# Attention weights times V as three float32r products of split operands, in place of one float32 product

## The chip, the core and the metric

The kernel runs on one core of one Trainium2 chip. The metric is the device time of one execution in microseconds (us). Engines are named as in the profile: PE (TensorE matmul), PEld (its weight load), DVE (VectorE), ACT (ScalarE), POOL (GpSimd), SP (SyncE, which issues the DMAs).

## The reference

Two layers of a decoder trunk on 256 tokens of width 1024, all in float32. Each layer projects the normed input into three branches (a gated depthwise convolution of 31 taps, a sparse attention, a short gated convolution), merges them with gates, and ends with a feed-forward block. The part that matters here is the attention, for each block of 128 queries:

```python
logits = jnp.einsum('btgrd,btkgd->btgrk', qg, kg).astype(jnp.float32) * scale
logits = jnp.where(valid[:, :, None, None, :], logits, -jnp.inf)
p = jax.nn.softmax(logits, axis=-1).astype(v.dtype)
o = jnp.einsum('btgrk,btkgd->btgrd', p, vg)
```

There are 8 query heads in 2 groups, each group with one key and one value head of 128 columns.

## The kernel before

**Streams.** The weights arrive as chunks of 2048 columns by 128 rows. Each chunk is cut into two halves of 1024 columns. ACT rounds a half to float32r (`cast`, L429, tile `wh`), DVE subtracts that from the original (`low`, through `vtt`, L386, tile `wl`). There are six buffers of `wh` and six of `wl`. The activations are split in the same way, and each product with a weight tile is three float32r matmuls: high by high, low by high, high by low. A half of 1024 columns holds 8 tiles and so feeds 24 matmuls of 256 columns. Each layer takes 180 halves; 90 of them come before the stage `T` of the layer.

**Stages of a layer**, in the order of the weights: `A` (convolution branch in), `IQ`, `KX`, `V`, `Q` (attention in), `C`, `CB`, `S` (short branch), `G` (gates), `T` (attention out), `F` (convolution branch out), `O`, `U`, `N` (feed-forward). Beside them run the convolution (`acc`, 31 taps on DVE with a third of the taps prepared by ACT as `ct`) and the attention itself, both fed into the other stages' gaps.

**Order.** No order is left to the hardware: `Plan.schedule` gives every instruction a cost and a due time, and on each engine takes next, among the instructions that are ready at that moment, the one with the smallest due time. It puts out one fixed order for each engine. The due time of a matmul group is the running sum `clk["t"]` of PE costs; that of a weight half's `cast` and `low` is `clk["t"] - LEAD` (9 us before its use); that of all convolution taps is one constant, the layer's start plus `CONVDUE` (150 us); attention steps get a due time of their own, advanced by `spend`.

**Attention loop.** For each of 2 query blocks `b` and 2 groups `g` there are: float32 products `qk`, a masked row maximum on DVE (L968, `lgt`), the softmax on ACT, a transposition on PE of each key block (`tp`, L367; one key block for `b`=0, two for `b`=1), an ACT copy of it to SBUF (`pT`), and the product with V:

```python
po = G.buf([P, 4, P], "pa", f"po{l}_{b}_{g}")
pe([mm(po, vt[:, kb, g * P:(g + 1) * P], pT[kb], kb == 0, kb == b, 512, True)
    for kb in range(b + 1)])
act(ah[:, hs, bq], po, AF.Copy)
low(al[:, hs, bq], po, ah[:, hs, bq])
```

Each product has 128 rows and 512 columns. Over both layers there are 12: per layer one for each of the two groups of `b`=0, two for each group of `b`=1. The result `ah`, `al` is read by stage `T`. `vt` is an ACT copy of the V projection. Line numbers of helpers: L369 is every matmul, L386 `vtt`, L393 `vstt` (convolution taps and others), L424 `act`, L429 `cast`.

Of the kernel before, what the change touches and what calls it, by code (L numbers as in the profile page):

```python
# [10 lines left out]
F32R = mybir.dt.float32r  # L11
I32 = mybir.dt.int32
AF = mybir.ActivationFunctionType
# [3 lines left out]
P = 128  # L17
D = 1024
S = 256
# [40 lines left out]
for _n, _w in (("ident", 128), ("caus0", 128), ("caus1", 256), ("cosq", 32), ("sinq", 32),  # L60
# [4 lines left out]

SLOTS = {"raw": 3, "wh": 6, "wl": 6, "big": 8, "att": 2, "pm": 4, "pq": 2, "pa": 2,
         "m1": 5, "m2": 3, "rr": 3, "b1": 2, "b2": 2, "lgt": 1, "rel": 2, "rope": 4, "junk": 1,
         "m8": 2, "tv": 3, "ty": 3, "tt": 3, "r2": 2, "two": 7, "one": 9, "mx": 2, "sm": 2, "ri": 2}
SHARED = {"m1": ("one", 5), "rr": ("one", 3), "b1": ("one", 2), "m2": ("two", 3), "rel": ("two", 2), "b2": ("two", 2), "ct": ("two", 2)}
BANKS = ("pm", "pq", "pa")  # L70
LAYOUT = (["gap40"] + [f"big_{i}" for i in range(8)] + [f"att_{i}" for i in range(2)] + ["kT_0", "vt_0"],
# [68 lines left out]
def ap_of(x):  # L140
    return x.ap() if isinstance(x, View) else x
# [198 lines left out]
def trunk(ctx: ExitStack, tc: tile.TileContext, xt: bass.AP, wst: bass.AP, prm: bass.AP,  # L340
# [7 lines left out]
    G = Plan()  # L348
    clk = {"t": 0.0}

    def width(v):
        if isinstance(v, View) and not v.whole:
            return v.n
        raise ValueError

    def pe(mms, due=None):
        outs, ins, cost = {}, {}, 0.0
        for o, l, r, st, sp, n, full, kw in mms:
            outs[id(o)] = o
            ins[id(l)] = l  # L360
            ins[id(r)] = r
            cost += max(4 * (n / 2.4 + 1.2), 218) if full else max(n, 256) / 2.4 + 2.4

        def fn():
            for o, l, r, st, sp, n, full, kw in mms:
                if kw == "t":
                    nc.tensor.transpose(ap_of(o), ap_of(l), ap_of(r))  # L367
                else:
                    nc.tensor.matmul(ap_of(o), ap_of(l), ap_of(r), start=st, stop=sp, skip_group_check=bool(kw))  # L369

        G.add("pe", fn, list(outs.values()), list(ins.values()), cost, due=due)
        return cost

    def mm(o, l, r, st, sp, n, full=False, kw=None):
        return (o, l, r, st, sp, n, full, kw)

    def tr(o, i):
        return (o, i, ident, True, True, P, False, "t")

    def psum(v):  # L380
        return isinstance(v, View) and v.buf.tag in BANKS

    def vtt(o, a, b, op, n=None):
        n = n or width(o)
        c = 62 if psum(a) or psum(b) or psum(o) else 66
        G.add("dve", lambda: nc.vector.tensor_tensor(ap_of(o), ap_of(a), ap_of(b), op=op), [o], [a, b], (c + n) / 0.96)  # L386
# [20 lines left out]
    def act(o, i, f, scale=None, bias=None, accum=None, n=None):  # L407
        n = n or width(o)
        cost = n / 1.2 + (51 if psum(i) else 94)
        kw = {}  # L410
        ins = [i]
        outs = [o]
        for k, v in (("scale", scale), ("bias", bias)):
            if v is not None:
                kw[k] = v
                ins.append(v)
                cost += 93
        if accum is not None:
            kw["accum_out"] = accum
            outs.append(accum)  # L420
            cost += 93

        def fn():
            nc.scalar.activation(ap_of(o), ap_of(i), f, **{k: ap_of(v) for k, v in kw.items()})  # L424

        G.add("act", fn, outs, ins, cost, func=f)
# [8 lines left out]
    def low(o, full, hi):  # L435
        vtt(o, full, hi.bitcast(F32), ALU.subtract)
# [16 lines left out]
    def big(name, dt=F32, tag="big"):  # L453
        return G.buf([P, 8, S], tag, name, dt)
# [91 lines left out]
    for k in range(KD):  # L546
        r, src = (r0, src0) if k < 4 else (r1, src1)
        dma(r[:, 512 * (k % 4):512 * (k % 4 + 1)], src[:, 512 * (k % 4):512 * (k % 4 + 1)], 256, -9e5)
        if k in (0, 1, 2, 4, 6):
            w = 1 if k < 2 else 2  # L550
# [90 lines left out]
    def tok(name, xh, xl, n, chunks):  # L641
        one = n * 2 <= 512
        if one:
            t = G.buf([P, 2, n], "pm", name)
            ps = [t[:, b, :] for b in range(2)]
        else:
            t = [G.buf([P, n], "pm", f"{name}_{b}") for b in range(2)]
            ps = t
        per = KD // (2 * chunks)
        for c in range(chunks):  # L650
            base = 2 * W.c
            for k0 in range(2 * c * per, 2 * (c + 1) * per, per):
                h, l = W.get(base + k0 // per - 2 * c)
                g = []
                for k in range(k0, k0 + per):
                    o = k % per * n
                    for b in range(2):
                        sl = slice(b * P, (b + 1) * P)
                        st = k == 0 and (b == 0 or not one)
                        g.append(mm(ps[b], xh[k][:, sl], h[:, o:o + n], st, False, n, kw="s"))  # L660
                        g.append(mm(ps[b], xh[k][:, sl], l[:, o:o + n], False, False, n, kw="s"))
                        g.append(mm(ps[b], xl[k][:, sl], h[:, o:o + n], False, k == KD - 1, n, kw="s"))
                clk["t"] += pe(g, due=clk["t"])
            W.skip()
        G.due = clk["t"]
        return t
# [96 lines left out]
    for l in range(DEPTH):  # L763
# [38 lines left out]
        ikT = G.buf([P, S], "ikT", f"ikT{l}")  # L802
        iws = G.buf([P, 2, IH], "iws", f"iws{l}")
        kx = G.buf([P, 2, KX], "kx", f"kx{l}")
        vt = G.buf([P, 2, S], "vt", f"vt{l}")
        iqb = big(f"iq{l}")
        ssq = G.buf([P, 2, HEADS], "ssq", f"ssq{l}")
        rs = G.buf([P, 2, HEADS], "rs", f"rs{l}")
# [17 lines left out]
        for t in range(0, 4, 2):  # L826
            pt = G.buf([P, 2, S], "pq", f"tiq{l}_{t}")
# [4 lines left out]
        pt = G.buf([P, S], "pq", f"tik{l}")  # L832
# [16 lines left out]
        pt = G.buf([P, 2, S], "pa", f"tk{l}")  # L849
# [1 line left out]
        act(kT, pt, AF.Copy, scale=par("kgm"))  # L851

        psv = tok(f"V{l}", xh, xl, 256, 1)
        act(vt, psv, AF.Copy)

        qt = big(f"qt{l}")
        qr = qt.rearrange("p (b h) (u d) -> p b (h u) d", b=2, u=2)
# [2 lines left out]
        for g in range(2):  # L860
# [12 lines left out]
            for i in range(2):  # L873
                pt = G.buf([P, 2, S], "pa", f"tq{l}_{n + i}")
# [8 lines left out]
        def spend(ns):  # L883
            paced["t"] += ns * PACE
            G.due = paced["t"]

        for b in range(2):
            nk = (b + 1) * P
            one = (66 + nk) / 0.96
# [5 lines left out]
            g = []  # L895
# [8 lines left out]
            for c in range(4 // per):  # L904
                for i in range(2):
                    rl = G.buf([P, per, nk], "rel", f"rel{l}_{b}_{c}_{i}")
                    act(rl, pss[c][i], AF.Relu)
                    for u in range(per):
                        h = 2 * (per * c + u) + i
# [3 lines left out]
            for r in range(TOPK // 8):  # L913
                m8 = G.buf([P, 8], "m8", f"m8{l}_{b}_{r}")
# [34 lines left out]
        for b in range(2):  # L949
            nk = (b + 1) * P  # L950
            one = (66 + nk) / 0.96
            bq = slice(b * P, (b + 1) * P)
            for g in range(2):
                G.due = paced["t"]
                mx = G.buf([P, 4], "mx", f"mx{l}_{b}_{g}")
                sm = G.buf([P, 4], "sm", f"sm{l}_{b}_{g}")
                ri = G.buf([P, 4], "ri", f"ri{l}_{b}_{g}")
                lgt = G.buf([P, 4, nk], "lgt", f"lgt{l}_{b}_{g}")
                hs = slice(4 * g, 4 * g + 4)
                pss = []  # L960
                for hp in range(2):
                    ps = G.buf([P, 2, nk], "pq", f"qk{l}_{b}_{g}_{hp}")
                    pe([mm(ps[:, i, :], qT[:, 4 * g + 2 * hp + i, bq], kT[:, g, :nk], True, True, nk, True)
                        for i in range(2)])
                    for i in range(2):
                        u = 2 * hp + i
                        G.add("dve", lambda o=lgt[:, u, :], i=ps[:, i, :], m=mx[:, u:u + 1], bb=bias[b]:
                              nc.vector.tensor_tensor_reduce(ap_of(o), ap_of(i), ap_of(bb), 1.0, GONE,  # L968
                                                             ALU.add, ALU.max, ap_of(m)),
                              [lgt[:, u, :], mx[:, u:u + 1]], [ps[:, i, :], bias[b]], one)  # L970
                spend(4 * one)
                vstt(mx, mx, -1.0, rs[:, b, hs], ALU.mult, ALU.mult)
                for u in range(4):
                    act(lgt[:, u, :], lgt[:, u, :], AF.Exp, scale=rs[:, b, 4 * g + u:4 * g + u + 1],
                        bias=mx[:, u:u + 1], accum=sm[:, u:u + 1])
                G.add("dve", lambda ri=ri, sm=sm: nc.vector.reciprocal(ap_of(ri), ap_of(sm)), [ri], [sm], 100)
                for u in range(4):
                    act(lgt[:, u, :], lgt[:, u, :], AF.Copy, scale=ri[:, u:u + 1])
                spend(500)
                pT = []  # L980
                for kb in range(b + 1):
                    pt = G.buf([P, 4, P], "pa", f"tp{l}_{b}_{g}_{kb}")
                    pe([tr(pt[:, u, :], lgt[:, u, kb * P:(kb + 1) * P]) for u in range(4)])
                    s = G.buf([P, 4, P], "b2", f"pT{l}_{b}_{g}_{kb}")
                    act(s, pt, AF.Copy)
                    pT.append(s)
                spend(500)
                po = G.buf([P, 4, P], "pa", f"po{l}_{b}_{g}")
                pe([mm(po, vt[:, kb, g * P:(g + 1) * P], pT[kb], kb == 0, kb == b, 512, True)
                    for kb in range(b + 1)])  # L990
                act(ah[:, hs, bq], po, AF.Copy)
                low(al[:, hs, bq], po, ah[:, hs, bq])
                spend(700)
# [224 lines left out]
```

## Time and profile before

| what | value |
|---|---|
| median of 3 runs | 1032.6 us (1032.03 to 1032.61) |
| the profiled execution, its own time | 1033.92 us |
| its span, first to last instruction | 1032.1 us |
| granted TensorE clock | 1.00 of full speed throughout |
| PE / PEld / DVE / ACT busy | 1025.4 / 1003.1 / 910.3 / 697.6 us |

The span is 1.8 us shorter than the execution's own time; what lies outside it is not touched. The busy time of PE is a modelled one: matmuls overlap, so a matmul that shows 276 ns may follow the one before it after 113 ns. What a matmul costs is therefore read from runs of many, as the chain gives them, by dividing time by count. The same holds for DVE, where the next instruction may begin before the one before it has ended: the distance between starts is what an instruction costs.

### The profile page before, as it was taken

The page shows a single profiled execution, that of the slowest core. Times are in us where ns is not written, and L with a number is a line of the kernel's source. Part 1 is how long each engine was busy: PE and PEld are TensorE (multiplying, and loading weights), DVE is VectorE, ACT ScalarE, POOL GpSimd, SP SyncE. Part 2 cuts the span into 40 slices and gives each one's busy share as a digit, 9 for nine tenths or more (in the row PEclk, how much of TensorE's full clock was granted, in tenths as well). Part 3 has the DMA queues.
Part 4 walks back from the last instruction along what each step waited for, and adds up shares of the span by engine and source line. Part 5 has one row for each costly group of instructions (what it writes and reads, how often), then busy time and mean ns, then how long its engine had stood idle before and what let it go on. Part 6 is the DMA issues. An engine that isn't in the chain of part 4 may idle for free.

```text
span 1032.1 us, 21274 instructions
## 1 busy us (share of the span) xinstructions
PE 1025.4 (99%) x8584; PEld 1003.1 (97%) x8584; DVE 910.3 (88%) x1805; ACT 697.6 (68%) x1228; POOL 0.2 (0%) x4
## 2 busy tenths in 40 slices
PE   8999999999999999999999999999999999999998
PEld 8998999999999999999999989999999999999998
DVE  6999999999998899885689999999998789998742
ACT  6878758896566676665476796588957466776531
POOL 0000000000000000000000000000000000000000
PEclk9999999999999999999999999999999999999999
DMA  8564445345665356555545544643564653655550
GB/s 307 204 235 185 166 160 173 123 159 169 238 207 204 124 204 227 196 206 200 182 173 195 205 161 160 210 159 124 170 238 164 211 198 128 226 220 193 186 215 21
DMA packets 29187, 191.59 MB, mean 186 GB/s; under 512 B 3232, under 2 KB 4512, under 8 KB 6816
## 3 DMA queue, kind: packets, MB, share of 16 engines
q1 hardware_dynamic: 28656, 189.70, 52.2%
q8 instruction: 67, 1.10, 0.4%
q10 hardware_dynamic: 432, 0.53, 0.2%
q14 instruction: 32, 0.26, 0.1%
HBM read 189.17 MB, written 1.05 MB: 184 GB/s over the span
## 4 chain that ended last, share of the span: by engine, by line
PE 96%; DVE 2%; DMA 1%; ACT 0%; issue 0%; ACTq 0%; SPq 0%
PE U L369 23%; PE G L369 13%; PE N L369 12%; PE C L369 9%; PE A L369 6%; PE Q L369 4%; PE T L369 4%; PE S L369 4%; PE CB L369 4%; PE O L369 4%; PE F L369 4%; PE IQ L369 2%; PE KX L369 1%; PE V L369 1%; PE qk L369 1%; PE po L369 1%
## 5 line engine op out<-in xcount | busy, mean ns | idle before, releaser
L386 DVE TENSOR_TENSOR wl<-raw,wh 128x1024 fp32r<-128x1024 f32 (+2 forms) x364 | 433.8, 1201 | 62.7 <-ACT wh L429 62.0
L429 ACT CAST wh<-raw 128x1024 fp32r<-128x1024 f32 (+2 forms) x364 | 369.5, 1030 | 139.2 <-PE N L369 37.1
L369 PE MATMUL U<-hhb,wh 128*128 128x256 f32 x576 | 134.1, 276 | 0.0
L369 PE MATMUL U<-hhb,wl 128*128 128x256 f32 x576 | 134.1, 276 | 0.0
L393 DVE SCALAR_TENSOR_TENSOR acc<-a,psb,acc 128x246 f32<-128x246 f32 (+16 forms) x320 | 132.4, 464 | 0.2
L369 PEld LDWEIGHTS U<-hhb,wh 128*128 128x128 f32 x576 | 108.1, 188 | 0.0
L369 PEld LDWEIGHTS U<-hhb,wl 128*128 128x128 f32 x576 | 108.1, 188 | 0.0
L369 PE MATMUL G<-hha,wh 128*128 128x256 f32 x384 | 90.4, 278 | 0.0
L369 PE MATMUL G<-hha,wl 128*128 128x256 f32 x384 | 89.7, 276 | 0.0
L369 PE MATMUL N<-uh,wh 128*128 128x256 f32 x352 | 80.7, 276 | 0.0
L369 PE MATMUL N<-uh,wl 128*128 128x256 f32 x352 | 80.7, 276 | 0.0
L369 PE MATMUL U<-hlb,wh 128*128 128x256 f32 x576 | 77.0, 276 | 0.0
L393 DVE SCALAR_TENSOR_TENSOR u<-U,psb,u 128x255 f32<-128x255 f32 (+1 forms) x144 | 59.7, 475 | 14.4 <-ACT u L424 14.4
L369 PEld LDWEIGHTS G<-hha,wl 128*128 128x128 f32 x384 | 72.1, 188 | 0.2 <-issue 0.2
L369 PEld LDWEIGHTS G<-hha,wh 128*128 128x128 f32 x384 | 72.1, 188 | 0.2 <-issue 0.2
L369 PEld LDWEIGHTS U<-hlb,wh 128*128 128x128 f32 x576 | 70.6, 188 | 0.0
L424 ACT ACTIVATE ct<-a,psb 128x253 f32<-128x253 f32 (+9 forms) x160 | 70.2, 488 | 0.0
L369 PEld LDWEIGHTS N<-uh,wh 128*128 128x128 f32 x352 | 66.1, 188 | 0.0
L369 PEld LDWEIGHTS N<-uh,wl 128*128 128x128 f32 x352 | 66.1, 188 | 0.0
L369 PE MATMUL C<-hha,wh 128*128 128x256 f32 x256 | 60.6, 279 | 0.0
L369 PE MATMUL C<-hha,wl 128*128 128x256 f32 x256 | 60.0, 276 | 0.0
L424 ACT ACTIVATE u<-U,psb 128x256 f32<-128x256 f32 x72 | 37.3, 560 | 27.3 <-PE U L369 27.3
(255 smaller groups left out, 2487.5 us busy)
## 6 DMA issues: line engine op xcount, KB each, us to landing
raw<-in_w SPq DMA_DIRECT2D x174, 1024.0 KB, 4.8
raw<-in_w SPq DMA_DIRECT2D x4, 656.0 KB, 3.8
raw<-in_w SPq DMA_DIRECT2D x8, 256.0 KB, 5.2
out<-xres SPq DMA_DIRECT2D x8, 128.0 KB, 2.8
psb<-in_p SPq DMA_DIRECT2D x2, 277.0 KB, 6.7
xres<-in_xt SPq DMA_DIRECT2D x2, 256.0 KB, 4.9
csb<-in_c SPq DMA_DIRECT2D x1, 304.0 KB, 8.9
xres<-in_xt ACTq DMA_DIRECT2D x1, 256.0 KB, 6.8
```

The costliest lines, as they stand in the source:

```text
L369: nc.tensor.matmul(ap_of(o), ap_of(l), ap_of(r), start=st, stop=sp, skip_group_check=bool(kw))
L386: G.add("dve", lambda: nc.vector.tensor_tensor(ap_of(o), ap_of(a), ap_of(b), op=op), [o], [a, b], (c + n) / 0.96)
L393: G.add("dve", lambda: nc.vector.scalar_tensor_tensor(ap_of(o), ap_of(a), ap_of(s), ap_of(b), op0=op0, op1=op1), [o], [a, s, b], (c + n) / ...
L424: nc.scalar.activation(ap_of(o), ap_of(i), f, **{k: ap_of(v) for k, v in kw.items()})
L429: G.add("act", lambda: nc.scalar.copy(ap_of(o), ap_of(i)), [o], [i], width(o) / 1.2 + 94)
```

## The change

V and the transposed softmax weights are each split into a float32r part and the rest, as the weights and activations already are, and the float32 product becomes three float32r products into the same PSUM tile. The V projection's copy is now the high part, and DVE makes the low part `vl` (a subtraction of 512 columns, once a layer). The ACT copy of each transposed block is now its high part, and DVE makes its low part from PSUM (512 columns, once for each key block). Two buffers `pl` and one `vl` are new in SBUF. No DMA is touched.

```diff
-         "m8": 2, "tv": 3, ...
+         "m8": 2, "pl": 2, "tv": 3, ...
...
-        vt = G.buf([P, 2, S], "vt", f"vt{l}")
+        vh = G.buf([P, 2, S], "vt", f"vh{l}", F32R)
+        vl = G.buf([P, 2, S], "vl", f"vl{l}", F32R)
...
-        act(vt, psv, AF.Copy)
+        act(vh, psv, AF.Copy)
+        low(vl, psv, vh)
...
-                    s = G.buf([P, 4, P], "b2", f"pT{l}_{b}_{g}_{kb}")
-                    act(s, pt, AF.Copy)
-                    pT.append(s)
+                    h = G.buf([P, 4, P], "b2", f"pTh{l}_{b}_{g}_{kb}", F32R)
+                    w = G.buf([P, 4, P], "pl", f"pTl{l}_{b}_{g}_{kb}", F32R)
+                    act(h, pt, AF.Copy)
+                    low(w, pt, h)
+                    pT.append((h, w))
...
-                pe([mm(po, vt[:, kb, g * P:(g + 1) * P], pT[kb], kb == 0, kb == b, 512, True)
-                    for kb in range(b + 1)])
+                gs = slice(g * P, (g + 1) * P)
+                mms = []
+                for kb in range(b + 1):
+                    h, w = pT[kb]
+                    mms.append(mm(po, vh[:, kb, gs], h, kb == 0, False, 512))
+                    mms.append(mm(po, vl[:, kb, gs], h, False, False, 512))
+                    mms.append(mm(po, vh[:, kb, gs], w, False, kb == b, 512))
+                pe(mms)
```

## Rows read from the trace of the kernel before

**Rows 1.** The page: busy time of each engine, and the chain by engine.
```profile
PE 1025.4 (99%) x8584; PEld 1003.1 (97%) x8584; DVE 910.3 (88%) x1805; ACT 697.6 (68%) x1228; POOL 0.2 (0%) x4
...
PE 96%; DVE 2%; DMA 1%; ACT 0%; issue 0%; ACTq 0%; SPq 0%
```

**Rows 2.** Waits before PE, first and last of four (us in total, times, longest).
```profile
PE A L369 <- ACT xgha L424: 1.1, 1, 1.1
...
PE A L369 <- DVE wl L386: 0.6, 2, 0.4
```

**Rows 3.** Instructions on the tile po: ns min/median/max, first and last start.
```profile
L369 PE MATMUL po<-pT,vt x24: 590/592/592, 171.3 to 742.3; 128*128 128x512 f32 x24
```

**Rows 4.** Timeline of PE around one product of layer 0: start, length, instruction.
```profile
171.26 1.02 PE L369 MATMUL po<-pT,vt 128*128 128x512 f32 x2
...
172.23 0.28 PE L369 MATMUL CB<-hha,wl 128*128 128x256 f32 x1
```

**Rows 5.** The chain in order of time, three pieces: start, length, matmul count.
```profile
72.26 2.80 PE V L369 x24
...
78.96 10.97 PE Q L369 x48
...
347.14 112.48 PE U L369 x992
```

**Rows 6.** Engines' busy us in stretches of layer 0 (PE, PEld, DVE, ACT).
```profile
80.00:90.00 10.00, 10.00 (x47) 8.21 (x46) 9.48 (x20) 7.75 (x15) 0.00 (x0) 1.00 0.51 179
...
160.00:205.00 45.00, 45.00 (x373) 43.63 (x373) 44.83 (x106) 38.83 (x87) 0.00 (x0) 1.00 0.41 141
...
231.00:262.00 31.00, 31.00 (x276) 31.00 (x275) 30.75 (x53) 19.68 (x31) 0.00 (x0) 1.00 0.50 173
```

**Rows 7.** Timeline of DVE in layer 0: start, length, instruction, [idle before].
```profile
209.69 0.69 DVE L386 TENSOR_TENSOR al<-po,ah 128x512 fp32r<-128x512 f32 x1
210.29 0.64 DVE L386 TENSOR_TENSOR acc<-acc,ct 128x470 f32<-128x470 f32 x1
...
212.76 1.23 DVE L386 TENSOR_TENSOR wl<-raw,wh 128x1024 fp32r<-128x1024 f32 x1
...
231.25 0.69 DVE L386 TENSOR_TENSOR al<-po,ah 128x512 fp32r<-128x512 f32 x1 [0.83 <-ACT ah L424]
...
243.31 1.22 DVE L386 TENSOR_TENSOR wl<-raw,wh 128x1024 fp32r<-128x1024 f32 x1
...
245.95 0.68 DVE L386 TENSOR_TENSOR mg<-g,mg 128x512 f32<-128x512 f32 x1
...
247.11 1.22 DVE L386 TENSOR_TENSOR wl<-raw,wh 128x1024 fp32r<-128x1024 f32 x1
...
259.54 1.22 DVE L386 TENSOR_TENSOR wl<-raw,wh 128x1024 fp32r<-128x1024 f32 x1
...
293.95 0.75 DVE L386 TENSOR_TENSOR cfl<-lu,cfh 128x256 fp32r<-128x256 f32 x2
```

**Rows 8.** The chain in layer 0 from the third attention step to stage T.
```profile
207.93 18.14 PE G L369 x160
...
230.58 35.36 PE G L369 x312
...
266.37 6.38 PE G L369 x56
272.75 3.63 PE T L369 x32
```

**Rows 9.** The chain in layer 1, first gate run and start of stage T.
```profile
715.76 20.86 PE G L369 x184
...
782.77 1.81 PE T L369 x16
```

**Rows 10.** Timeline of DVE in layer 1 at the same place.
```profile
716.42 0.69 DVE L386 TENSOR_TENSOR al<-po,ah 128x512 fp32r<-128x512 f32 x1 [0.72 <-ACT ah L424]
...
724.58 1.22 DVE L386 TENSOR_TENSOR wl<-raw,wh 128x1024 fp32r<-128x1024 f32 x1
```

More of the change, by code (lines that the diff above doesn't have):

```diff
@@ L67 @@
          "m1": 5, "m2": 3, "rr": 3, "b1": 2, "b2": 2, "lgt": 1, "rel": 2, "rope": 4, "junk": 1,
-         "m8": 2, "tv": 3, "ty": 3, "tt": 3, "r2": 2, "two": 7, "one": 9, "mx": 2, "sm": 2, "ri": 2}
+         "m8": 2, "pl": 2, "tv": 3, "ty": 3, "tt": 3, "r2": 2, "two": 7, "one": 9, "mx": 2, "sm": 2, "ri": 2}
 SHARED = {"m1": ("one", 5), "rr": ("one", 3), "b1": ("one", 2), "m2": ("two", 3), "rel": ("two", 2), "b2": ("two", 2), "ct": ("two", 2)}
```

## The prediction, before the change was run

> **What bounds the kernel now.** I read the page first, then who waited for whom, then the chain of waits, and last the timelines of DVE and PE side by side. The page and the chain say PE: 99% busy, 96% of the chain [rows 1]. The waits before PE are four, and both rows shown are of stage A; none lies behind the first stage [rows 2]. From there to the end PE runs without a gap, so a microsecond of matmul taken away is a microsecond of the whole, as long as PE's operands stay ahead. That condition is the question here, for DVE, which makes the low half of every weight, is full in the very stretch that the change touches: 44.83 of 45 us from 160 on and 30.75 of 31 from 231 on [rows 6].
>
> How far ahead is DVE? The trace doesn't number the halves, but they can be counted back from stage T. A half feeds 24 matmuls, 24 x 0.1134 = 2.72 us (0.1134 = 112.48 / 992, [rows 5]). 90 halves precede T, the first four of them written in two pieces each, so T's first half is the 95th `wl` write; that of 259.54 us is the 91st, four halves before T: 96 G matmuls. Of these 56 run from 266.37 us and 40 end the run before, which ends at 230.58 + 35.36 = 265.94 [rows 8]. The first reads at 265.94 - 40 x 0.1134 = 261.4 us. The DVE instruction ends at 259.54 + 1.22 = 260.76 [rows 7]. **The lead is 0.6 us.** The same count for the `wl` of 212.76 us (20 halves, 480 of the 544 G matmuls from 207.93 on, so read at 207.93 + 64 x 0.1134 = 215.2, written by 213.99): 1.2 us [rows 7, 8]. In layer 1 the smallest lead in this stretch is that of 724.58 us: 19 halves before T, 456 of the 560 G matmuls between 715.76 and 782.77, so read at 715.76 + 104 x 0.1134 = 727.55, written by 725.80: 1.7 us [rows 9, 10]. So PE is the bound with DVE directly behind it.
>
> **What the change takes from PE.** A float32 product shows as two matmul instructions [rows 3]. The pair starts at 171.26, and the second matmul behind it at 172.23, one of 0.113 after the first [rows 4]: the product holds PE for 0.86 us. Over 12 products that is 10.3 us. The three float32r products of 512 columns have no row of their own with these operands. The nearest is stage Q, also 512 columns of float32r: 10.97 / 48 = 0.2285 [rows 5]. The bounds: a quarter of the float32 product, 0.2145, and twice stage V's 256 columns, 2 x 2.80 / 24 = 0.233. With 0.2285 a product becomes 0.686, saves 0.174, and 12 save **2.1 us** (bounds 1.9 to 2.6). Stage U would say 2 x 0.1134, inside them.
>
> The Trainium skill ("FP8 and Floating Point Precision", TensorE Precision Notes) says that true float32 takes four passes through the array, and reduced precision reads the value cut to 22 bits in one. By that rule alone three passes cost three quarters, which saves 12 x 0.215 = 2.6 us. The trace agrees in kind, but stage Q's pass is slower than a float32 pass, so I take the smaller figure.
>
> **What it adds to DVE.** Per layer six lows of transposed weights and one of V, each a subtraction of 512 columns with a PSUM operand. The same shape and kind stands in the trace as `al`: 0.69 us long, 0.60 from start to start (209.69 to 210.29, [rows 7]). So 14 x 0.60 = 8.4 us. The V low comes at about 80 us, where DVE was idle for 0.52 us of ten [rows 6]; I cost it at nothing, and at 0.6 if that cover is gone. The six others fall between 168 and 231 us in layer 0, and at the corresponding place in layer 1.
>
> The Trainium skill ("VectorE: DVE Perf Modes", § TRN2 errata) gives (N+151)/0.96 ns for a float32 tensor_tensor, 0.69 us at 512 columns, and its tier table leaves float32 tensor_tensor in the slowest mode. The trace's length agrees; by the page's figure the sum would be 14 x 0.69 = 9.7 us, and the six in a layer would weigh 0.5 us more, but the distance between starts is what the queue pays.
>
> Who is behind them? Due times decide. The attention's due times are smaller than those of the weight halves used at the time, and the convolution's one due time is past, so `wl` comes last: it gets a turn only where a convolution step waits for the one before it. The row of `mg` at 245.95 between two `wl` shows another step taking such a turn [rows 7]. The lows will go ahead of `wl`, not behind.
>
> **ACT, buffers, the new wait.** ACT does the same copies in another output type: nothing. `po` now waits for a DVE low behind the ACT copy, 0.6 us plus whatever DVE has in hand (a `wl`, 1.13). Behind `po` on PE stand gate matmuls of the fixed order; the planner places `po` after the low's planned end, so I cost this at nothing, and at 8 x 1.7 = 14 us if all eight steps ran into it. `ah` is not needed before T, some 40 us later. `pl` and `vl` touch no transfer.
>
> **The sum.** Layer 0: by 259.54 six lows have gone ahead, 6 x 0.60 = 3.6 us; the lead covers 0.6, and the idle 0.83 us ahead of `al` at 231.25 [rows 7] may or may not absorb some, since the new lows wait for PE in the same way. PE is late by 2.2 to 3.0 us, I take 2.6. The 1.05 us that PE saves in this layer is gone too, because PE then waits for DVE whatever it did before. At 215.2 us four lows against 1.2 us already give 1.2 us of this. Past that point it is not lost twice: the convolution branch's last low (293.95, ends 294.70, [rows 7]) is read only in the fifth microsecond of F, and F begins later as well.
>
> Layer 1: at 724.58 four lows are ahead, 2.4 us, against a lead of 1.7 and an idle 0.72 [rows 10]: PE late by 0 to 0.7. Then the last two products give 0.35 back: -0.35 to +0.35, I take 0. Between the layers DVE recovers.
>
> Together +2.6 us (1.85 to 3.35): 1032.1 + 2.6 = 1034.7 of span, 1036.5 for the profiled execution with its 1.8 us outside the span. That execution lies 1.3 us above the median of the runs, so against the median: **1035.2 us**.
>
> **The rivals.**
>
> *The saving stays* (faster). If the planner leaves the weight halves ahead, PE keeps its 2.1 us: 1030.5 (1030.0 to 1030.7). For it: PE waits for nothing now [rows 2], and convolution steps could go later. It decides only if about 3.6 us of convolution (nine taps) moves behind the halves read at 215 and 261 us. Against it: the convolution's due time is past. Chance 0.20.
>
> *The two cancel.* The planner hides about half of the lows; PE waits 0.2 to 2.9 us in all and saves 2.1: 1030.7 to 1033.4. Chance 0.17.
>
> *The lows take turns, not only time.* Each low that takes a gap between two dependent convolution steps sends the `wl` there to the next gap; `wl` of 243.31 to the next at 247.11 shows 3.8 us where `mg` took one [rows 7], about 2.2 us each way without it. Two lows in front of the half at 215 and two in front of those after 231 then cost 4 to 7 us in layer 0 and up to 2 in layer 1: 1036.7 to 1041.5, the middle 1038.5. Against it: if PE is late, the gate steps come later too and free their turns. Chance 0.18.
>
> *The forecast*, DVE late by the plain sum of its work. Its bottom is 1.2 us of lateness at the half read at 215 alone, less 0.35 in layer 1: 1033.4. Its top is 3.35 and an uncovered V low of 0.6: 1036.6. Chance 0.45.
>
> **How the numbers follow.** 0.2% of 1032.6 is 2.1 us, about what a measurement of this kernel can tell from no change. The saving by itself sits on that edge: of its 0.20, 0.11 is faster and 0.09 the same. The cancelling case is the same (0.17). The forecast lies beyond 1034.7 in three parts of five: 0.27 slower, 0.18 the same. The last rival is slower. In all 0.11 faster, 0.44 the same, 0.45 slower. The range leaves out about a tenth at either end: 1030.3 cuts the lower half of the saving's case, 1038.5 the upper half of the last rival's. The forecast's own range is 1033.4 to 1036.6.
>
> **What would show it.** Right: waits of PE for `wl` in stages S or G of layer 0 between 190 and 262 us, 2 to 4 us in sum, none or few in layer 1; 36 `po` matmuls 0.21 to 0.235 us apart; 14 more DVE subtractions 0.60 apart. Wrong: no wait of PE behind stage A (the saving stays), or waits of 5 us and more with `wl` several turns later (the last rival), or `po` itself waiting for its low, which would make it slower at another place.

## The result and the profile after

The changed kernel takes **1040.2 us** (median of 4, 1038.54 to 1040.42); beside it the kernel before took 1032.61 (4 runs, 1032.03 to 1032.91). The ratio is 1.0067, interval 1.0055 to 1.0080: slower by 7.6 us, where 1035.2 was forecast with a range up to 1038.5. The profiled execution took 1040.42 us, its span is 1038.6.

The page of the changed kernel, busy times and chain, against [rows 1]:

```profile
PE 1027.2 (99%) x8596; PEld 1009.5 (97%) x8596; DVE 917.7 (88%) x1819; ACT 698.7 (67%) x1228; POOL 0.2 (0%) x4
...
PE 82%; DVE 14%; ACT 3%; issue 1%; DMA 0%; DVEq 0%; ACTq 0%
```

PE has the 12 new matmuls and DVE the 14 new subtractions (7.4 us more). The busy shares hardly move; the chain does: DVE goes from 2% of it to 14%. The waits before PE, against [rows 2], say where:

```profile
PE G L369 <- DVE wl L386: 6.1, 4, 2.2
PE A L369 <- ACT xgha L424: 1.2, 1, 1.2
PE pw L369 <- DVE avg L535: 1.0, 1, 1.0
```

Four waits of stage G for the low half of a weight, 6.1 us, which the kernel before did not have. The chains of both kernels give the stretch in which the time is lost: the first piece of V (before's first one is in [rows 5]) and of F in each layer, before and then after.

```profile
295.46 21.76 PE F L369 x192
...
581.99 2.81 PE V L369 x24
...
805.02 21.76 PE F L369 x192
```

```profile
70.71 2.81 PE V L369 x24
...
298.33 21.76 PE F L369 x192
...
584.86 2.80 PE V L369 x24
...
811.53 21.76 PE F L369 x192
```

From V to F the kernel before needs 295.46 - 72.26 = 223.20 us in layer 0 and 805.02 - 581.99 = 223.03 in layer 1; the changed one 227.62 and 226.67. That is **+4.42 and +3.64**. From F to the next V both need 286.53. So everything is lost between V and F, where the attention is. (The profiled execution of before began V 1.55 us later, which is why the spans differ by 6.5 and not by 8.1.)

**The mechanism, half by half.** DVE in layer 0, against [rows 7]: the stretch between two turns of `wl`.

```profile
204.43 1.21 DVE L386 TENSOR_TENSOR wl<-raw,wh 128x1024 fp32r<-128x1024 f32 x1
205.56 0.64 DVE L386 TENSOR_TENSOR acc<-acc,ct 128x482 f32<-128x482 f32 x1
206.13 0.67 DVE L386 TENSOR_TENSOR pTl<-tp,pTh 128x512 fp32r<-128x512 f32 x1
206.73 1.58 DVE L393 SCALAR_TENSOR_TENSOR acc<-a,psb,acc 128x240 f32<-128x240 f32 x4
208.24 0.67 DVE L386 TENSOR_TENSOR pTl<-tp,pTh 128x512 fp32r<-128x512 f32 x1
208.84 0.63 DVE L386 TENSOR_TENSOR acc<-acc,ct 128x476 f32<-128x476 f32 x1
209.41 0.41 DVE L970 CUSTOM_DVE_ANT_0 lgt<-qk,bias 128x256 f32<-128x256 f32 x1
...
214.00 0.68 DVE L386 TENSOR_TENSOR al<-po,ah 128x512 fp32r<-128x512 f32 x1
214.60 0.62 DVE L386 TENSOR_TENSOR acc<-acc,ct 128x464 f32<-128x464 f32 x1
215.15 0.41 DVE L970 CUSTOM_DVE_ANT_0 lgt<-qk,bias 128x256 f32<-128x256 f32 x1
...
215.49 1.55 DVE L393 SCALAR_TENSOR_TENSOR acc<-a,psb,acc 128x231 f32<-128x231 f32 x4
216.97 0.14 DVE L393 SCALAR_TENSOR_TENSOR mx<-mx,rs 128x4 f32<-128x4 f32 x1
217.04 1.21 DVE L386 TENSOR_TENSOR wl<-raw,wh 128x1024 fp32r<-128x1024 f32 x1
```

Convolution steps (`acc`) alternate with the others: what is not convolution gets a turn between two of them. The two lows take the turns at 206.13 and 208.24, the row maxima `lgt` and `al` the next ones, and `wl` comes at 217.04, 11.4 us behind the end of the one before. In the kernel before, the same half (by the count of `wl` writes; 19 halves ahead of T's first) was written here:

```profile
213.89 0.64 DVE L386 TENSOR_TENSOR acc<-acc,ct 128x464 f32<-128x464 f32 x1
214.44 1.23 DVE L386 TENSOR_TENSOR wl<-raw,wh 128x1024 fp32r<-128x1024 f32 x1
```

It took the turn right behind the `acc` of 464 columns. In the changed kernel that turn went to the last `lgt` (215.15), so `wl` stands behind the 231-column step as well. Counted from the start of V, `wl` ends at 214.44 + 1.23 - 72.26 = 143.4 before and at 217.04 + 1.21 - 70.71 = 147.5 after: 4.1 us later, of which the four lows of transposed weights ahead of it make 2.4 and the extra convolution step 1.5 (215.49 to 216.97). PE reads it here, and stands:

```profile
216.01 0.28 PE L369 MATMUL G<-hha,wh 128*128 128x256 f32 x1
218.31 0.39 PE L369 MATMUL G<-hha,wl 128*128 128x256 f32 x1 [2.02 <-DVE wl L386]
```

The gap from 216.01 to 218.31 is 2.30, less one matmul of 0.11: 2.2 us lost. In the same way 1.5 us are lost at 223.74 and 0.7 at 252.36. In layer 1 it is sharper. DVE there, first before (this half stood ahead of the attention's block; the next one, at 724.58 in [rows 10], behind it), then after:

```profile
711.20 1.22 DVE L386 TENSOR_TENSOR wl<-raw,wh 128x1024 fp32r<-128x1024 f32 x1
```

```profile
709.97 1.22 DVE L386 TENSOR_TENSOR wl<-raw,wh 128x1024 fp32r<-128x1024 f32 x1
...
722.96 1.22 DVE L386 TENSOR_TENSOR wl<-raw,wh 128x1024 fp32r<-128x1024 f32 x1
...
728.34 1.22 DVE L386 TENSOR_TENSOR wl<-raw,wh 128x1024 fp32r<-128x1024 f32 x1
```

The half that the kernel before wrote at 711.20 (the same by the count of writes), 129.2 us after V's start, is now that of 728.34, 143.5 us after it: some 14 us later, for four lows of 0.60 ahead of it. Two halves have fallen to the far side of the attention's block. PE needs this one at 727.28:

```profile
727.17 0.28 PE L369 MATMUL G<-hha,wh 128*128 128x256 f32 x1
729.61 0.38 PE L369 MATMUL G<-hha,wl 128*128 128x256 f32 x1 [2.16 <-DVE wl L386]
...
730.99 0.41 PE L369 MATMUL G<-hha,wl 128*128 128x256 f32 x1
731.21 0.41 PE L369 MATMUL G<-hha,wh 128*128 128x256 f32 x1
```

Behind this wait of 2.3 us the matmuls are 0.21 us apart (730.99 to 731.21) and not 0.113. The windows show why; the column behind the five busy times is the granted clock:

```profile
727.00:729.50 2.50, 0.45 (x4) 0.25 (x3) 2.50 (x7) 2.11 (x3) 0.00 (x0) 1.00 0.53 220
729.50:733.50 4.00, 3.89 (x20) 3.89 (x21) 4.00 (x8) 4.00 (x12) 0.00 (x0) 0.59 0.30 61
733.50:738.00 4.50, 4.50 (x41) 4.50 (x40) 4.50 (x9) 4.48 (x8) 0.00 (x0) 0.99 0.65 238
```

0.59 over the window: for most of it the clock was at the lower of its two levels, 1.2 GHz, behind the wait of PE. From 730.17 to 733.93 PE does 19 matmuls; at 0.1134 they would take 2.15 us, so PE is slower by 1.6 us here. Whether the whole is longer by as much is a question for the second profile, further down.

The new products themselves: two key blocks of `po` in the chain, six matmuls.

```profile
746.16 1.39 PE po L369 x6
```

1.39 / 6 = 0.232 each, where 0.2285 was taken.

### The profile page after: what moved, and what is told of

It reads as the page before. It is cut to its first block, busy times and chain, and to the rows that moved or that the text cites. A ratio compares the mean times of both kernels' runs of the same rounds, so it can differ in the third digit from the quotient of the medians.

```text
span 1038.6 us, 21303 instructions
## 1 busy us (share of the span) xinstructions
PE 1027.2 (99%) x8596; PEld 1009.5 (97%) x8596; DVE 917.7 (88%) x1819; ACT 698.7 (67%) x1228; POOL 0.2 (0%) x4
## 4 chain that ended last, share of the span: by engine, by line
PE 82%; DVE 14%; ACT 3%; issue 1%; DMA 0%; DVEq 0%; ACTq 0%
PE U L369 23%; PE N L369 12%; PE A L369 9%; PE G L369 8%; PE C L369 4%; PE T L369 4%; PE O L369 4%; PE F L369 4%; DVE acc L393 4%; DVE wl L386 4%; PE Q L369 3%; PE IQ L369 2%; PE CB L369 2%; PE S L369 2%; DVE acc L386 2%
## 5 line engine op out<-in xcount | busy, mean ns | idle before, releaser
L393 DVE SCALAR_TENSOR_TENSOR acc<-a,psb,acc 128x246 f32<-128x246 f32 (+17 forms) x320 | 131.6, 461 | 0.1
L369 PE MATMUL G<-hha,wl 128*128 128x256 f32 x384 | 91.8, 280 | 6.1 <-DVE wl L386 6.1
```

The source lines that it names most:

```text
L393: G.add("dve", lambda: nc.vector.scalar_tensor_tensor(ap_of(o), ap_of(a), ap_of(s), ap_of(b), op0=op0, op1=op1), [o], [a, s, b], (c + n) / ...
```

## The experiments

Three theories. **A:** the lows take turns of the weight halves in DVE's fixed order, so a half loses more than the low's length. **B:** DVE is late by the plain sum of the lows' time, the forecast's mechanism. **C:** the products, or the new tiles and waits around them, are slow themselves. The medians, and the two stretches from V to F read from each chain as above:

| kernel | median us (range, runs) | before beside it | ratio (interval) | V to F, layers 0 and 1 |
|---|---|---|---|---|
| e1_no_lows | 1030.5 (1030.29–1031.82, 10) | 1032.58 | 0.9981 (0.9971–0.9991) | 222.43, 222.10 |
| e2_lows_only | 1037.04 (1036.76–1037.77, 4) | 1032.58 | 1.0043 (1.0028–1.0058) | 227.00, 224.13 |
| e9_short_lows | 1036.71 (1036.38–1037.16, 4) | 1032.58 | 1.0039 (1.0024–1.0054) | 226.34, 224.09 |
| e10_unplanned_lows | 1035.33 (1034.82–1036.09, 7) | 1032.58 | 1.0025 (1.0014–1.0036) | 225.83, 223.11 |
| e3_lows_b0 | 1033.29 (1032.44–1034.06, 10) | 1032.43 | 1.0007 (0.9998–1.0016) | 224.26, 222.35 |
| e4_lows_b1 | 1035.12 (1034.83–1037.12, 7) | 1032.43 | 1.0029 (1.0018–1.0039) | 225.90, 223.17 |
| e6_cact12 | 1031.52 (1030.77–1032.41, 11) | 1032.43 | 0.9992 (0.9983–1.0001) | 222.39, 222.76 |
| e7_convdue165 | 1033.05 (1032.59–1034.06, 10) | 1032.43 | 1.0006 (0.9997–1.0015) | 223.21, 222.66 (PE timeline) |
| e11_cact12_pace36 | 1032.21 (1031.71–1034.2, 11) | 1032.39 | 1.0000 (0.9991–1.0008) | 222.97, 222.88 |
| e8_before_same_constants | 1033.2 (1032.74–1035.31, 11) | 1032.39 | 1.0008 (0.9999–1.0017) | 223.27, 223.85 |
| e12_after_again | 1040.48 (1039.8–1043.08, 4) | 1032.39 | 1.0074 (1.0059–1.0090) | 228.06, 226.68 |
| e13_cact12_low_due30 | 1031.16 (1030.68–1032.74, 11) | 1032.78 | 0.9986 (0.9977–0.9995) | 222.87, 222.10 |

**The products without the lows.** e1_no_lows, against the changed kernel:

```diff
-        low(vl, psv, vh)
...
-                    low(w, pt, h)
-                    pT.append((h, w))
+                    pT.append((h, h))
...
-                    mms.append(mm(po, vl[:, kb, gs], h, False, False, 512))
+                    mms.append(mm(po, vh[:, kb, gs], h, False, False, 512))
```

> All low parts of V and of the transposed weights are left out; the three products are made of the high parts, so PE does the same 36 products and DVE nothing more. Theory A (the lows push weight halves to later turns of DVE) and theory B (the lows cost DVE 0.60 us each, in plain sum): no wait of PE for a weight half in the gate stages, and the products' own saving, 10.3 - 36 x 0.231 = 2.0 us: about 1030.6 us. Theory C (the three products or the new tiles themselves are what is slow): near 1040.

Measured 1030.5: 2.1 us faster than before, the forecast's PE saving (its two stretches show 1.7), and PE waits for no weight half behind stage A. C falls for the products; the new tiles are not in this kernel, but they are in e6 and e7 below, which lose nothing like it. The lows cost 1040.2 - 1030.5 = 9.7 us.

**The lows without the products.** e2_lows_only is the kernel before with its float32 product, and the lows beside it, read by nobody:

```diff
+        low(vl, psv, vt)
...
+                    w = G.buf([P, 4, P], "pl", f"pTl{l}_{b}_{g}_{kb}", F32R)
                     act(s, pt, AF.Copy)
+                    low(w, pt, s)
```

> The kernel before, with its float32 product, and the 14 lows made beside it and read by nobody. Theory A: the lows take turns as in the changed kernel, PE waits 4 to 7 us for weight halves, 1036 to 1042 us. Theory B: 3 to 4 us of lateness, nothing saved: 1035.5 to 1036.5. Theory C: as before, 1032.6.

Measured 1037.04, 4.5 us slower than before, with three waits for `wl` (2.7 us in sum, the longest 1.3). It lies in A's range and 0.5 us above B's. The lows make a loss without the products. Why it is smaller than the 9.7 above was not tested: PE lacks the saving here, and the order is another.

**The turns without the time.** e9_short_lows keeps the changed kernel's order, instruction for instruction, with the planner's cost of a low unchanged, but each low of the transposed weights does one column, and the third product reads the high part:

```diff
-                    low(w, pt, h)
+                    c = View(w.buf, (lambda t: t[:, 0, 0:1],), w.idx)
...
+                    vtt(c, p1, h1, ALU.subtract, n=512)
+                    w.ap = h.ap
```

> The changed kernel in its own order, instruction for instruction, but each low of the transposed weights writes one column in place of 512 (some 0.07 us in place of 0.60), and the third product reads the high part. So DVE's order stays and the lows' time goes. Theory A: the four waits of PE stay, each up to 1 us shorter: 1036 to 1039 us. Theory B: without the lows' time the waits go: 1030.6 to 1031.5.

**The time without the turns.** e10_unplanned_lows does the lows in full, but tells the planner that they cost 1 ns:

```diff
-                    low(w, pt, h)
+                    G.add("dve", lambda ...: nc.vector.tensor_tensor(
+                        ..., op=ALU.subtract), [w], [pt, h.bitcast(F32)], 1.0)
```

> The changed kernel with the full lows of the transposed weights, but the planner is told that they cost nothing, so that they take no turn from a weight half in its order; on the chip they take their 0.60 us each. Theory A: the large waits go, what is left is some 1 to 3 us: 1031 to 1034. Theory B: lateness by the plain sum, 2.2 to 3.0 us in layer 0 and none in layer 1: 1034.5 to 1036, or as the changed kernel, 1040.

The waits of the two, of e9 first:

```profile
PE G L369 <- DVE wl L386: 4.1, 4, 1.3
```

```profile
PE G L369 <- DVE wl L386: 1.4, 2, 0.8
...
PE po L369 <- DVE pTl L989: 0.2, 1, 0.2
```

e9 takes 1036.71: a low that lasts 0.15 us on the chip and has its place in the order still costs 6.2 us over e1. The halves written at 217.04 and 218.73 in the changed kernel come at 216.26 and 217.95 here, a mere 0.8 earlier. Part of the time that the lows give up is lost again, for the order is fixed: DVE stands 0.33 us ahead of `al` at 182.35 and 0.45 at 213.21, waiting for ACT's `ah`, where the changed kernel has no such gap. Counted from V the first of the two halves ends at 216.26 + 1.22 - 71.00 = 146.5, still 3.1 us later than before. That is A, bare: with most of the lows' time gone, the order makes PE wait at the same four places. e10 takes 1035.33: the time alone costs 4.8 over e1, 225.83 - 223.20 = +2.6 us in layer 0 and +0.1 in layer 1 against before. The timeline shows what the planner did: both lows of a group run in one turn, at 206.43 and 207.03 us, where the changed kernel has a convolution step between them, and the half that was 4.1 us late there is written at 216.09 here and ends 216.09 + 1.23 - 71.72 = 145.6 after V's start: 2.2 later than before, about the four lows' 2.4. A's range for e10 (1031 to 1034) is missed, B's (1034.5 to 1036) met. These are the forecast's terms and, within 0.1 us, its time, though PE waits at 229 and 233 us and not at 215 and 261, so how close it comes is in part luck. B's sum fits lows that take time and no turns of their own; the kernel's lows also take turns. 6.2 and 4.8 make 11.0 and not 9.7: the two overlap, and how they share the loss isn't settled.

**Half of the lows.** e3_lows_b0 has V's lows and those of `b`=0, e4_lows_b1 only those of `b`=1; the others are left out as in e1.

```diff
-                    low(w, pt, h)
+                    w = h
+                    if b == 0:      # e4: b == 1
+                        ...
+                        low(w, pt, h)
```

> The changed kernel with the lows of V and of the first query block's transposed weights alone (two of six in a layer); the second block's are left out and its third product reads the high part. Theory A (what counts is which turn a low takes, and how far ahead the weight halves are there): these lows run near 170 and 180 us, where the halves lead by 9 to 14 us, so little is lost: 1030.5 to 1032.5 us, no wait near 216. Theory B (plain sum of time, wherever it falls): a third of the changed kernel's loss of 9.7 us over the lows-free one, 1033.7.

> The other four of six: lows of the second query block's transposed weights alone; V's and the first block's are left out and high parts read in their place. Theory A: nearly all of the loss, since these fall where the halves lead by 1 to 5 us: 1034 to 1039 us, waits in both layers' gate stages. Theory B: two thirds of the loss, 1037.

2.8 and 4.6 us over e1. e3 came near B's number and missed A's: lows of `b`=0 have one wait behind them (1.5 us). e4 met A's range and lies 1.9 us below B's number; it waits four times, 3.0 us in sum. Together they make 7.4 of the 9.7: all the lows at once cost more than the two parts added up.

**Other turns for the same work.** e6_cact12 has ACT prepare two more convolution taps a layer (`ct`); e7_convdue165 lets the convolution be due 15 us later, so that `wl` goes ahead of it where both are ready, and changes no instruction of the kernel.

```diff
-CACT = 10
+CACT = 12              # e6
-CONVDUE = 150000.0
+CONVDUE = 165000.0     # e7
```

> The changed kernel, complete, with 12 in place of 10 of the 30 convolution taps prepared by ACT (CACT). A pair of taps costs DVE 0.57 us in place of 2 x 0.38, so DVE gets 8 x 0.19 = 1.5 us back in each layer and ACT gets 8 x 0.85 = 6.8 us more. If the loss is DVE being late with weight halves (A or B), most of the waits go and the saving shows: 1030.5 to 1034 us. If it were the products or the tiles (C, already unlikely), 1040.

> The changed kernel, complete, with the convolution's due time 15 us later (CONVDUE 165 in place of 150 us). Not a microsecond of work is taken away; only the turns change: weight halves go before convolution taps for longer. Theory A: the waits near 216, 223 and 727 us go; what is left is at the end of the convolution or before stage F: 1030.5 to 1034 us. Theory B: the work is the same, so is the lateness: 1035 to 1040.

No wait for `wl` in stage G is left in either. On PE and DVE e7 does the same instructions as the changed kernel, in another order, and takes 7.2 us less (1033.05 against 1040.2). (ACT has four table loads fewer in this order. They are not the cause: in the changed kernel DVE is busy for 151.88 of the 152 us from 110 to 262, so it was not waiting for ACT there.) C falls with it, for all the new tiles and waits are in e6 and e7. Which work stands ahead of `wl` decides, and not how much work there is. A sum of what stands ahead of a half could still allow that; together with e9, where the sum is small and the waits stay, B falls as the explanation of the changed kernel. What e7 pays is seen at F, which now waits for the convolution branch:

```profile
PE F L369 <- ACT cfh L424: 0.7, 1, 0.7
```

From F to the next V it needs 287.57 us where all others need 286.53. The interval of e6 touches 1, so it is not told apart from before.

**Can the saving be kept?** Three runs: e11_cact12_pace36 (CACT 12, and attention steps due a little later, PACE 3.6 for 3.5), e8_before_same_constants (the kernel before with the same two constants), and e13_cact12_low_due30: CACT 12, and the lows of the transposed weights due 30 us later, so that they yield to `wl`:

```diff
-CACT = 10
+CACT = 12
...
+                    keep, G.due = G.due, G.due + 30000
                     low(w, pt, h)
+                    G.due = keep
```

> The changed kernel, complete, with 12 taps on ACT and the attention's due times advanced a little faster (PACE 3.6 in place of 3.5), so that its steps fall on other turns. If lateness of weight halves is the whole loss, and both constants leave it small, PE's saving shows: 1030.6 to 1031.5 us, and against the kernel before a ratio of 0.998 to 0.999 with an interval below 1. If a loss comes with the lows whatever the order (plain sum, theory B), not under 1033.

> The control: the kernel before with the same two constants. It has no waits of PE behind the first stage that the constants could remove, so 1032.0 to 1033.5 us. Were it faster than that, the gain of the run beside it would be the constants' and not the three products'.

> The changed kernel, complete, with 12 taps on ACT and the lows of the transposed weights due 30 us later, so that on DVE they no longer go ahead of weight halves that PE reads soon. If lateness is the whole loss, the time is that of the run with 12 taps or up to 0.5 us better, 1030.8 to 1031.6 us, with an interval below 1 against the kernel before; no wait of PE for a weight half in the gate stages. If a loss comes with the lows whatever the order, not under 1033.

e11 missed its expectation: no wait for `wl` behind stage A, yet the same time as before. e8 shows that the constants are no help to the kernel before. With these constants in both kernels the change is the faster one by 1.0 us (medians of 11 runs each, 1032.21 against 1033.2; an interval for this pair was not worked out). e13 has one wait for `wl` in stage G, of 0.3 us:

```profile
PE G L369 <- DVE wl L386: 0.3, 1, 0.3
```

It takes 1031.16, faster than before by 0.14% (interval 0.05% to 0.23%) and by 9 us than the change as made. In the profile its stretches are those of e1 but for 0.4 us, with all 14 lows in. The kernel before with CACT 12 alone was not run, so what of the 1.6 us is CACT's is open.

**The changed kernel once more.**

> The changed kernel, nothing edited, profiled a second time. The waits of PE for weight halves near 216, 223, 252 and 727 us are in its order and come again, 2.0, 1.4, 0.6 and 2.2 us. The stretch at half the granted clock behind the last of them need not come again: if it is the wait that brings it, it stands behind one of the waits of 2 us, and costs 1.6 us there; without it this profile's time is 1.6 us lower, 1038 to 1039.

1040.48. The windows of its stage G in layer 0, with the clock as above:

```profile
218.00:220.50 2.50, 0.49 (x6) 0.29 (x4) 2.50 (x7) 1.42 (x2) 0.00 (x0) 1.00 0.00 0
220.50:224.00 3.50, 3.50 (x16) 3.50 (x17) 3.50 (x7) 3.49 (x12) 0.00 (x0) 0.51 0.65 229
224.00:228.00 4.00, 4.00 (x37) 4.00 (x36) 4.00 (x9) 3.97 (x8) 0.00 (x0) 1.00 0.15 64
```

0.51 in the window behind the wait at 218.2; behind that at 729.8 the clock is halved again. In the first profile only layer 1 had it. Of the four expected waits three came; the one near 223, of 1.5 us in the first profile, did not:

```profile
PE G L369 <- DVE wl L386: 4.7, 3, 2.2
```

PE reached that half later at half the clock and found it written. From the last matmul ahead of the first wait to the start of T it takes 277.64 - 218.21 = 59.43 us here, with the half clock, and 275.45 - 216.01 = 59.44 in the first profile, without it: in layer 0 the half clock cost nothing, because DVE's lateness at the next half took its place. (This execution is the longest of its four. V begins 72.92 - 70.71 = 2.2 us later than in the first profile, which is most of the difference.)

## Why the prediction was wrong

**What bounds the kernel** was right: PE with DVE directly behind it, and the chain now passes through DVE 14% of the way. So was the warning that the lows go ahead of `wl` and not behind.

**What the change takes from PE** was right: 2.1 us forecast, 2.1 in e1 between the medians, 1.7 in its profile (446.23 - 444.53 from V to F). A product takes 3 x 0.232 = 0.70 us instead of 0.86, a ratio of 0.81. By the four-pass rule of the Trainium skill ("FP8 and Floating Point Precision", TensorE Precision Notes) it would be 0.75; the measurement decides for the smaller saving, as the prediction did.

**The price of a low**, 0.60 from start to start, was right (206.13 to 206.73).

**`po`'s own wait** was costed at nothing and cost next to nothing: one wait behind a low, 0.2 us in e10, and 0.4 ahead of one weight load in the tile's list of the changed kernel.

**The sum is the step that failed.** It added six lows of 0.60, took the lead of 0.6 off, and for layer 1 let a lead of 1.7 us cover 2.4 us of lows. That prices a low by its length. Layer 0 lost 4.42 and not 2.6, layer 1 3.64 and not 0; 8.06 - 2.6 = 5.5 us more than the sum; the median lies 5.0 above the forecast. What happened instead is the rival *The lows take turns, not only time*, with a chance of 0.18 and a range of 1036.7 to 1041.5, which holds the result; its sign, waits of 5 us and more, came too (6.1). Its price for layer 0 (4 to 7) was right; that for layer 1 (up to 2) was too low against 3.64, of which 1.6 are PE at half the clock. What spoke against it, that gate steps come later with PE and free their turns, did not save the first late half: what stands ahead of it are steps of the attention, `lgt` and `al`, in an order that is fixed before the run.

**The places.** The count of leads was right in its method and led to the wrong halves: 215 and 261 us in layer 0 and 727 in layer 1 were named, and PE waited at 216, 224, 252 and 727. The leads were those of the old order. The planner made a new one, in which a half that had stood behind one convolution step stood behind two (216), and one that had stood ahead of the attention's block stood behind it (727). A lead says how much time a half can lose; it says nothing of how much it loses when its turn goes.

**The clock** was in no step. In both profiles PE is slower by 1.6 us in layer 1 for it. How much of the median it makes is open: the four executions of e12 had mean clocks of 0.997, 0.999, 0.997 and 1.0 of full speed at 1043.08, 1039.8, 1040.71 and 1040.25 us, and the last is not the shortest. In layer 0 of e12 a DVE late at the next half took back all that a full clock would have given; whether it would in layer 1 no run shows.

**The range** reached to 1038.5, the middle of that rival, because its upper half was left out with a tenth of the chance.

## What to carry to other kernels

Where an engine is full, price an added instruction by the turn that it takes: find which instruction stood there, the next place it can go to, and how far ahead its reader is; here four subtractions of 0.60 us put a weight half 14 us later. If the added work is needed late, say so in its due time: other due times were worth 7 us here with the same instructions (e7), and 9 together with two taps moved to ACT (e13). And a lead read from the old order is only good for the old order.

## What the runs showed of the hardware that was not expected

PE lost half its clock behind waits of 2.0 to 2.2 us in an otherwise dense stream. Of the four such waits in the two profiles of the changed kernel three had it (218.2 and 729.8 in e12, 727.2 in the first profile), and the one at 216.0 of the first profile had not; nor had the shorter waits of e2, e9, e10, e3 and e4 (at most 1.5 us). Between starts a 256-column matmul then took 0.213 us and not 0.113. The Trainium skill ("TensorE: Matmul & The Clock Gate", Part 1) says that the clock gate passes one of two rates, half or full, by how busy PE has lately been; the trace agrees with the two rates (0.51 in the window that lies almost wholly inside such a stretch, 1.00 on either side). Why the wait at 216.0 kept its clock, no run here shows.
